# adaLN sums as a moving operand on four column groups, three more adaLN chunks on GpSimd, and the softmax scaling of head pairs placed inside the recurrence

## The chip, the cores and the metric

The kernel runs on one core of one Trainium2 chip. The metric is the device time of one execution in microseconds. A core has five engines, each with its own in-order instruction stream: TensorE (PE; its weight loads are shown as PEld), VectorE (DVE), ScalarE (ACT), GpSimd (POOL) and SyncE (SP), which here issues most of the DMAs. [...]

## The reference

One step of one trunk layer, over 1024 latent tokens and 256 context tokens, model width 1024, all in float32. The parts that the change touches:

```python
m = silu(cond) @ w_ada + b_ada                       # adaLN: 6 vectors of 1024, for two conds (c and c_ctx)
h = rms_norm(x) * (1 + sc1) + sh1
z = h @ w_in                                         # 5376 columns: recurrence, attention and gate inputs
o_a = softmax(q k^T / 8) v                           # 8 heads of 64, two kv heads; latents also see 512 cached keys
o_h = hgrn(...)                                      # gated linear recurrence, 4 heads of 128, forward and backward
merged = sigmoid(g0) * (o_h @ w_ho) + sigmoid(g1) * (o_a @ w_ao)
x = x + g1_ada * (merged @ w_out)
x = x + g2_ada * (relu(norm(x) @ w_ff1)**2 @ w_ff2)  # then a last RMSNorm
```

The six adaLN vectors need w_ada, 1024 x 6144, times two condition vectors. The softmax's division by its row sums can be done at any point between the product with v and the projection w_ao.

## The kernel before, in words

Tokens are cut in three tiles TT: t=0 and t=1 of 512 latents, t=2 of the 256 context tokens. Activations lie transposed, channels on partitions. Matrix products with weights are done as three products of high and low halves (`split` makes the halves: ACT writes the rounded one, DVE the rest; lines 312 and 313 in the profile).

The stages in order of time:

- **Front** (to about 100 us): adaLN chunks 0 to 15, first norm, the attention's own columns of w_in.
- **Attention** (to about 690 us): units of one head and 256 queries, a software pipeline of scores (L845), exponentials (L857), transposes of the probabilities (L877, split at L880) and products with v (L891, L892). Between the units' events a `Filler` runs other matmuls: ten groups of 256 columns of w_in for the recurrence, generated by `with_ada`. Six of the groups are made channel by channel (L345 to L347), four token by token (`tok`, L362 to L364). In program order the filler has reached a set share of its total, 250 us of its own estimate, at each event. A unit pair's output, two heads on 128 partitions and not yet divided by the row sums, goes to DRAM as OA[c][t], c = 0 to 3. The reciprocals of the row sums go to DRAM as RS (`sums_rows`), 80 rows.
- **Recurrence** (to about 990 us): 24 units, each a head, a direction and a tile, in the order (0,0), (0,1), (1,1), (1,0), (0,2), (1,2) of (direction, tile) for each head, so that units 0, 6, 12 and 18 are the first of a head. Loop step i does `prep` of unit i+1 (loads of uf, uq, uv, ug; two scans on DVE; products on DVE and POOL; its key product is held in `keyed`), then unit i's scores (L1122) and states (L1134), the output of unit i-1 (L1153, L1155), the transposes of unit i+1's keys (`keys_t`, L1111) and unit i-1's gate. Three more steps (LATE) end the loop. A second Filler runs the eight groups of the gates' columns of w_in between these.
- **Merge** (from about 1015 us): for the tiles in the order 0, 2, 1, loads of OH (the recurrence's outputs) and OA, the division of OA by the row sums (two row loads from RS, spread over 64 partitions each, and a DVE product, L1337), splits, then the products with w_hgrn_out and w_attn_out, gates, w_out, and the MLP.

adaLN chunks 16 to 47 are made in pairs (ci, ci+1: 256 columns of w_ada, a 1 MB load into `wraw`, a pool of two buffers). Up to ci=32, nine chunks, GpSimd multiplies and adds the eight rows of 128 (`ada_sum`, L197 to L204) into two accumulators, ACC, one for each cond; ACC exists once. Then four TensorE matmuls with the accumulators as weights and a column of ones as the moving operand add over the partitions (L210), and DVE adds the bias (L212). This happens once in each group but the first: `ada_sum` is called at 0.25 of the group's work and the matmuls at 0.90, in the last group at 0.02 and 0.42. The seven chunks from 34 on are made on TensorE alone, in the recurrence: `ada_cols` (16 matmuls, L178, an ACT copy, a transpose, L184), one after each of the first seven gate groups.

What sets the order: TensorE's instructions stand in program order. The other engines' and the DMA queues' order is laid out by a list scheduler at compile time, which may move a load or a GpSimd chain far ahead of its place in the program when its buffers and inputs are there; `high_priority` and `issue_after` bend that order. At run time each engine and queue then keeps its order. Pools: ring X has 20 tiles of 128x512 and holds, in the recurrence, uf, uq, ucp, usf, uw, uv and ug of the units under way and later the merge's `or`; PSUM has 3 banks "g", 3 "s" and 2 "t". `R`, a mask that the scans need, takes the tile of `sums` (which holds ACC[0]) after the attention.

Of the kernel before, what the change touches and what calls it, by code (L numbers as in the profile page):

```python
# [15 lines left out]
P = 128  # L16
# [28 lines left out]
def build(ctx, tc, I, O, C):  # L45
# [54 lines left out]
    def dma(out, in_):  # L100
        return sp.dma_start(out=f32(out), in_=f32(in_))
# [91 lines left out]
    def ada_sum(ci, acc):  # L193

        raw = wraw(I["w_ada"], KC, ci * P)
        w = [ada_l[:, :, c:c + 1].broadcast_to([P, KC, 256]) for c in range(2)]
        g_.tensor_tensor(acc[0], raw[:, 0], w[0][:, 0], op=ALU.mult)  # L197
        for k in range(1, KC):
            g_.tensor_tensor(acc[1], raw[:, k], w[0][:, k], op=ALU.mult)
            g_.tensor_tensor(acc[0], acc[0], acc[1], op=ALU.add)  # L200
        g_.tensor_tensor(raw, raw, w[1], op=ALU.mult)
        for n in (4, 2):
            g_.tensor_tensor(raw[:, 0:n], raw[:, 0:n], raw[:, n:2 * n], op=ALU.add)
        g_.tensor_tensor(acc[1], raw[:, 0], raw[:, 1], op=ALU.add)  # L204

        def late():
            pt = PS("t")
            for b in range(2):
                for c in range(2):
                    pe.matmul(pt[:, 2 * c + b:2 * c + b + 1], acc[c][:, b * P:(b + 1) * P], ones, start=True, stop=True)  # L210
            with tc.high_priority(offset=600):
                v.tensor_tensor(modc[:, :, ci:ci + 2], pt[:, 0:4].rearrange("p (c b) -> p c b", c=2),  # L212
                                cols[:, B_ADA + ci:B_ADA + ci + 2].unsqueeze(1).broadcast_to([P, 2, 2]), op=ALU.add)
        return late


# [701 lines left out]
    def sums_rows():  # L918
# [4 lines left out]
        s_.activation(e, pt[0:80, 0:P], AF.Copy)  # L923
        dma(RS, e)

    gone, keyed, copied = [None], [None], [None]
    q_at, o_at = {}, {}
    K = [[[None] * 4 for _ in range(2)] for _ in range(2)]
# [259 lines left out]
    def hgrn(fill, before):  # L1188

        units = [HUnit(6 * h + j, h, d, t) for h in range(4) for j, (d, t) in enumerate(((0, 0), (0, 1), (1, 1), (1, 0), (0, 2), (1, 2)))]  # L1190
        fwd = {u.h: {} for u in units}
        for u in units:
            u.fwd = fwd[u.h].get(u.t)
            fwd[u.h][u.t] = u
        N, LATE = len(units), 3

        share = [u.n + 128.0 for u in units] + [300.0] * LATE
        tot, done, st = sum(share), 0.0, None
        with tc.issue_after(gone[0].ins):
            units[0].prep()  # L1200
        before()
        units[0].keys_t()
        for i in range(N + LATE):
            part = lambda x: fill.to((done + x * share[i]) / tot)
            if i + 1 < N:
                with ExitStack() as after:
                    after.enter_context(tc.issue_after(copied[0].ins))
                    after.enter_context(tc.issue_after(keyed[0].ins))
                    units[i + 1].prep()
            if i < N:  # L1210
                u = units[i]
                part(0.25)
                u.scores(u.fwd)
                part(0.5)
                u.states_(u.st or st)
                st = u.last
                if i == 0:
                    sums_rows()
                if u.t == 2:
                    store(O["new_state_hgrn"][u.d, u.h], st)  # L1220
                part(0.75)
            if i >= LATE and units[i - LATE].d == 1:
                units[i - LATE].out_t()
            if 1 <= i <= N:
                units[i - 1].out(units[i - 1].fwd)
            part(0.95)
            if i + 1 < N:
                units[i + 1].keys_t()
            if 1 <= i <= N and units[i - 1].d == 1:
                units[i - 1].gate(units[i + 1] if i + 1 < N else None)  # L1230
            part(1.0)
            done += share[i]
# [19 lines left out]
    def with_ada(groups, ahead, behind):  # L1252

        late = []
        for i, grp in enumerate(groups):
            nxt = groups[i + 1] if i + 1 < len(groups) else None
            at, acts = 0.0, []
            if i and ahead:
                ci = ahead.pop(0)
                t0, t1 = (0.25, 0.9) if nxt else (0.02, 0.42)  # L1260
                acts = [(t0, lambda: late.append(ada_sum(ci, ACC))), (t1, lambda: late.pop()())]
            for need, n, gen in grp.stages():
                if not grp.tok and need == (0,):
                    jobs = [(0.5, lambda: grp.part(1))]
# [19 lines left out]
        if todo:  # L1284
            todo.pop()()

    fz = Filler(with_ada([*zh(0), *zh(1)], list(range(16, 34, 2)), []), 250.0)
    while pending:
        fz.add(1.0)
        flush(1.0)  # L1290
# [4 lines left out]
    gls = [Group(GL + 256 * c, gl_consume(c), False) for c in range(8)]  # L1295
    with tc.high_priority(offset=600):
        gls[0].part(0)
    fg = Filler(with_ada(gls, [], list(range(34, 48, 2))), 196.0)
    hgrn(fg, fz.rest)
    fg.rest()  # L1300
    close("sl")
# [24 lines left out]
    for t in MT:  # L1326
        n = TT[t][1]
        for c in range(8):
            r = S(name="or")
            dma(r[:, 0:n], (OH if c < 4 else OA)[c % 4][t])  # L1330
            if c >= 4:
                q = S(name="or")
                for i in range(2):
                    r0 = 10 * (2 * (c - 4) + i) + TT[t][0] // P
                    row = RS[r0:r0 + n // P, :].rearrange("(o b) p -> o (b p)", o=1)
                    dma(q[64 * i:64 * i + 64, 0:n], row.broadcast_to([64, n]))
                v.tensor_tensor(r[:, 0:n], r[:, 0:n], q[:, 0:n], op=ALU.mult)  # L1337
            oT[t][c] = hpair(t)
            split(oT[t][c][0], oT[t][c][1], r[:, 0:n])
    mg = [[None] * KC for _ in range(3)]  # L1340
# [676 lines left out]
```

## Time and profile before

| | |
|---|---|
| median of 3 runs | 2040.8 us (2040.52 to 2042.02) |
| the profiled execution's own time | 2040.07 us |
| its span | 2038.3 us |
| PE busy | 2004.0 us, 98% of the span |
| PEld busy | 1734.4 us, 85% |
| DVE busy | 1346.3 us, 66% |
| ACT busy | 940.0 us, 46% |
| POOL busy | 526.7 us, 26% |
| granted TensorE clock | 0.999 |
| DMA | 320.00 MB, mean 157 GB/s |

The span is the time from the first to the last instruction of the profiled execution. A row of the timeline gives the start, the duration, the engine, the line, the operation, output<-inputs, the shapes and how many instructions are merged in it; in brackets the idle time of the engine before it and what ended that. A row of the waits gives who waited for whom, the total in us, how often, and the longest. SPq rows are DMA issues, not transfers.

### The profile page before, as it was taken

The page shows a single profiled execution, that of the slowest core. Times are in us where ns is not written, and L with a number is a line of the kernel's source. Part 1 is how long each engine was busy: PE and PEld are TensorE (multiplying, and loading weights), DVE is VectorE, ACT ScalarE, POOL GpSimd, SP SyncE. Part 2 cuts the span into 40 slices and gives each one's busy share as a digit, 9 for nine tenths or more (in the row PEclk, how much of TensorE's full clock was granted, in tenths as well). Part 3 has the DMA queues.
Part 4 walks back from the last instruction along what each step waited for, and adds up shares of the span by engine and source line. Part 5 has one row for each costly group of instructions (what it writes and reads, how often), then busy time and mean ns, then how long its engine had stood idle before and what let it go on. Part 6 is the DMA issues. An engine that isn't in the chain of part 4 may idle for free.

```text
span 2038.3 us, 33049 instructions
## 1 busy us (share of the span) xinstructions
PE 2004.0 (98%) x12246; PEld 1734.4 (85%) x12246; DVE 1346.3 (66%) x2474; ACT 940.0 (46%) x1965; POOL 526.7 (26%) x594
## 2 busy tenths in 40 slices
PE   7899999999999999999999999999999999999998
PEld 5698889988889988888878889988888888888886
DVE  5865665655665789877355635886666666577786
ACT  4635555555565423323312335755545544333443
POOL 1471321433303655544022101222112200000120
PEclk9999999999999999999999999999999999999999
DMA  9452211322122455554844424854454489455764
GB/s 317 155 193 83 81 58 47 105 93 76 38 92 80 149 158 175 160 176 149 249 145 143 170 104 148 258 183 146 146 164 145 147 309 357 135 166 171 237 236 138
DMA packets 222626, 320.00 MB, mean 157 GB/s; under 512 B 19161, under 2 KB 140801, under 8 KB 222465
## 3 DMA queue, kind: packets, MB, share of 16 engines
q1 hardware_dynamic: 209984, 277.99, 42.8%
q0 software_dynamic: 12480, 39.91, 5.3%
q8 instruction: 96, 1.57, 0.3%
q14 instruction: 66, 0.53, 0.1%
HBM read 232.05 MB, written 85.78 MB: 156 GB/s over the span
## 4 chain that ended last, share of the span: by engine, by line
PE 90%; DMA 4%; DVE 3%; ACT 1%; issue 1%; SPq 0%; POOL 0%; POOLq 0%; DVEq 0%; ACTq 0%
PE ps_g L345 8%; PE ps_g L346 7%; PE ps_g L347 7%; PE ps_s L845 4%; PE ps_t L877 4%; PE ps_g L362 2%; PE ps_g L892 2%; PE ps_g L364 2%; PE ps_g L363 2%; PE ps_g L1804 2%; PE ps_g L1806 2%; PE ps_g L1805 2%; PE ps_g L891 2%; PE ps_s L1649 2%; PE ps_s L1651 2%; PE ps_s L1650 2%
## 5 line engine op out<-in xcount | busy, mean ns | idle before, releaser
L345 PE MATMUL ps_g<-hs,wsp 128*128 128x512 f32 (+1 forms) x896 | 322.6, 360 | 0.0
L346 PE MATMUL ps_g<-hs,wsp 128*128 128x512 f32 (+1 forms) x896 | 309.2, 345 | 2.9 <-DVE hs L313 2.9
L347 PE MATMUL ps_g<-hs,wsp 128*128 128x512 f32 (+1 forms) x896 | 309.3, 345 | 0.0
L312 ACT ACTIVATE wsp<-wraw 128x512 fp32r<-128x512 f32 (+1 forms) x186 | 116.7, 668 | 208.4 <-PE ps_g L346 81.2
L846 DVE TENSOR_REDUCE mx<-ps_s 128x1 f32<-128x512 f32 (+1 forms) x208 | 138.1, 668 | 112.6 <-PE ps_s L845 110.6
L880 DVE TENSOR_TENSOR pTl<-ps_t,pTh 128x512 fp32r<-128x512 f32 x200 | 136.4, 684 | 88.0 <-ACT pTh L880 87.6
L313 DVE TENSOR_TENSOR wsp<-wraw,wsp 128x512 fp32r<-128x512 f32 (+1 forms) x186 | 147.4, 817 | 70.0 <-ACT wsp L312 69.7
L347 PEld LDWEIGHTS ps_g<-hs,wsp 128*128 128x128 f32 x896 | 169.3, 189 | 21.7
L345 PEld LDWEIGHTS ps_g<-hs,wsp 128*128 128x128 f32 x896 | 169.6, 189 | 20.3 <-issue 4.4
L346 PEld LDWEIGHTS ps_g<-hs,wsp 128*128 128x128 f32 x896 | 169.9, 190 | 18.2 <-DVE hs L313 3.4
L880 ACT ACTIVATE pTh<-ps_t 128x512 fp32r<-128x512 f32 x200 | 118.2, 602 | 139.3 <-PE ps_t L877 137.6
L312 ACT ACTIVATE ah<-ar 128x640 fp32r<-128x640 f32 (+1 forms) x112 | 80.9, 723 | 185.9 <-PE ps_g L1805 102.3
L857 ACT ACTIVATE pexp<-ps_s,ngm 128x512 f32<-128x512 f32 (+1 forms) x208 | 137.4, 669 | 42.7 <-DVE ngm L850 42.3
L313 DVE TENSOR_TENSOR ah<-ar,ah 128x640 fp32r<-128x640 f32 (+1 forms) x112 | 92.0, 822 | 78.2 <-ACT ah L312 77.8
L845 PE MATMUL ps_s<-Kl,Ql 128*128 128x512 f32 (+1 forms) x416 | 129.5, 411 | 0.0
L877 PE MATMUL ps_t<-ident,pexp 128*128 128x128 f32 x800 | 120.0, 272 | 0.1
L362 PE MATMUL ps_g<-wsp,hs 128*128 128x256 f32 x400 | 115.8, 289 | 0.0
L364 PE MATMUL ps_g<-wsp,hs 128*128 128x256 f32 x400 | 112.9, 282 | 0.0
L363 PE MATMUL ps_g<-wsp,hs 128*128 128x256 f32 x400 | 112.6, 281 | 0.0
L892 PE MATMUL ps_g<-pTl,Vl 128*128 128x256 f32 x400 | 104.2, 283 | 0.2
L891 PE MATMUL ps_g<-pTh,Vl 128*128 128x256 f32 x400 | 104.0, 281 | 0.0
L877 PEld LDWEIGHTS ps_t<-ident,pexp 128*128 128x128 f32 x800 | 94.4, 140 | 9.5 <-issue 0.6
(436 smaller groups left out, 5363.0 us busy)
## 6 DMA issues: line engine op xcount, KB each, us to landing
ar<-AF SPq DMA_DIRECT2D x112, 320.0 KB, 3.3
wraw<-in_w_ff SPq DMA_DIRECT2D x32, 1024.0 KB, 6.4
wr<-in_w_ff SPq DMA_DIRECT2D x128, 256.0 KB, 4.4
wraw<-in_w_in SPq DMA_DIRECT2D x18, 1024.0 KB, 5.6
wraw<-in_w_ada SPq DMA_DIRECT2D x16, 1024.0 KB, 5.4
AF<-a POOLq DMA_DIRECT2D x48, 256.0 KB, 2.7
AF<-t POOLq DMA_DIRECT2D x48, 256.0 KB, 2.3
wa<-in_w_ada SPq DMA_DIRECT2D x32, 256.0 KB, 5.9
```

Source lines behind the costliest of these rows:

```text
L312: s_.activation(hi, raw, AF.Copy)
L313: return v.tensor_tensor(lo, raw, f32(hi), op=ALU.subtract)
L345: pe.matmul(out, hi[:, k, :], mh, start=(first and k == 0), stop=False)
L346: pe.matmul(out, hi[:, k, :], ml, start=False, stop=False)
L347: pe.matmul(out, lo[:, k, :], mh, start=False, stop=(last and k == kcs - 1))
L362: pe.matmul(po[:, bb, :], mh[:, off:off + P], wh[:, k % 4, :], start=(k == 0), stop=False)
L363: pe.matmul(po[:, bb, :], mh[:, off:off + P], wl[:, k % 4, :], start=False, stop=False)
L364: pe.matmul(po[:, bb, :], ml[:, off:off + P], wh[:, k % 4, :], start=False, stop=(k == KC - 1))
L845: pe.matmul(pq[:, 0:n], self.qh[:, q0:q0 + P], K[self.g][var][self.kts[i]], start=(var == 0), stop=(var == 1))
L877: pe.transpose(pt[:, a, j * P:(j + 1) * P], self.Ps[j][i][:, b * P:(b + 1) * P], ident)
L880: behind[:] = s_.activation(hi, pt, AF.Copy), v.tensor_tensor(lo, pt, f32(hi), op=ALU.subtract)
L892: pe.matmul(pv[:, 0:256], V[self.g][kg][:, b, :], lo[:, a, :], start=False, stop=(k == last))
```

## The change

It has three parts.

1. `ada_sum`'s end: the accumulators become the moving operand (128 columns) and a column of ones spread to 32 columns becomes the weights, so that the four matmuls go to four column groups of the array. The sums then lie along the columns; ACT copies them to SBUF (`ev`, 128x128), and a second step, `last`, transposes them to where the old form had them, from a "t" bank of its own, and adds the bias. `with_ada` calls the two steps apart (0.45 and 0.49, or 0.93 and 0.97 of the group).
2. GpSimd makes twelve chunks (16 to 38) instead of nine, and TensorE's `ada_cols` four (40 to 46) instead of seven: in the four token groups `with_ada` now starts a chunk at 0.02 and another at 0.50 (the last group has the first alone). The second Filler's total goes from 196 to 190.
3. The division of OA by the row sums leaves the merge. `scale_pair` loads a pair's OA tile and its two rows in every odd step of the recurrence from i=3 on, ahead of `prep` of unit i+1; its second half, in the even step after it, multiplies behind that step's `keyed` on DVE and stores the result back to OA. The twelve pairs go in the order of tiles 0, 2, 1. The merge loads OA and splits it as it does OH.

```diff
--- before.py
+++ after.py
@@ -204,13 +204,19 @@
         g_.tensor_tensor(acc[1], raw[:, 0], raw[:, 1], op=ALU.add)
 
         def late():
-            pt = PS("t")
-            for b in range(2):
-                for c in range(2):
-                    pe.matmul(pt[:, 2 * c + b:2 * c + b + 1], acc[c][:, b * P:(b + 1) * P], ones, start=True, stop=True)
-            with tc.high_priority(offset=600):
-                v.tensor_tensor(modc[:, :, ci:ci + 2], pt[:, 0:4].rearrange("p (c b) -> p c b", c=2),
-                                cols[:, B_ADA + ci:B_ADA + ci + 2].unsqueeze(1).broadcast_to([P, 2, 2]), op=ALU.add)
+            pa = PS("t")
+            for q in range(4):
+                pe.matmul(pa[32 * q:32 * q + 32, 0:P], ones.broadcast_to([P, 32]), acc[q // 2][:, (q % 2) * P:(q % 2 + 1) * P], start=True, stop=True)
+            ev = S((P, P), name="ev")
+            s_.activation(ev, pa[:, 0:P], AF.Copy)
+
+            def last():
+                pt = PS("t")
+                pe.transpose(pt[:, 0:P], ev, ident)
+                with tc.high_priority(offset=600):
+                    v.tensor_tensor(modc[:, :, ci:ci + 2], pt[:, 0:P].rearrange("p (c b x) -> p c b x", c=2, b=2)[:, :, :, 0],
+                                    cols[:, B_ADA + ci:B_ADA + ci + 2].unsqueeze(1).broadcast_to([P, 2, 2]), op=ALU.add)
+            return last
         return late
 
 
@@ -923,6 +929,21 @@
         s_.activation(e, pt[0:80, 0:P], AF.Copy)
         dma(RS, e)
 
+    def scale_pair(c, t):
+
+        n = TT[t][1]
+        r, q = S(name="or"), S(name="or")
+        dma(r[:, 0:n], OA[c][t])
+        for i in range(2):
+            r0 = 10 * (2 * c + i) + TT[t][0] // P
+            row = RS[r0:r0 + n // P, :].rearrange("(o b) p -> o (b p)", o=1)
+            dma(q[64 * i:64 * i + 64, 0:n], row.broadcast_to([64, n]))
+
+        def late():
+            v.tensor_tensor(r[:, 0:n], r[:, 0:n], q[:, 0:n], op=ALU.mult)
+            dma(OA[c][t], r[:, 0:n])
+        return late
+
     gone, keyed, copied = [None], [None], [None]
     q_at, o_at = {}, {}
     K = [[[None] * 4 for _ in range(2)] for _ in range(2)]
@@ -1200,13 +1221,19 @@
             units[0].prep()
         before()
         units[0].keys_t()
+        pairs, scaled = [(c, t) for t in (0, 2, 1) for c in range(4)], []
         for i in range(N + LATE):
             part = lambda x: fill.to((done + x * share[i]) / tot)
+            if i > 2 and i % 2 and pairs:
+                scaled.append(scale_pair(*pairs.pop(0)))
             if i + 1 < N:
                 with ExitStack() as after:
                     after.enter_context(tc.issue_after(copied[0].ins))
                     after.enter_context(tc.issue_after(keyed[0].ins))
                     units[i + 1].prep()
+            if scaled and i % 2 == 0:
+                with tc.issue_after(keyed[0].ins):
+                    scaled.pop()()
             if i < N:
                 u = units[i]
                 part(0.25)
@@ -1256,9 +1283,14 @@
             nxt = groups[i + 1] if i + 1 < len(groups) else None
             at, acts = 0.0, []
             if i and ahead:
-                ci = ahead.pop(0)
-                t0, t1 = (0.25, 0.9) if nxt else (0.02, 0.42)
-                acts = [(t0, lambda: late.append(ada_sum(ci, ACC))), (t1, lambda: late.pop()())]
+                def begin():
+                    late.append(ada_sum(ahead.pop(0), ACC))
+
+                def end():
+                    late.append(late.pop()())
+                acts = [(0.02, begin), (0.45, end), (0.49, lambda: late.pop()())] if grp.tok else []
+                if nxt:
+                    acts += [(0.5 if grp.tok else 0.25, begin), (0.93, end), (0.97, lambda: late.pop()())]
             for need, n, gen in grp.stages():
                 if not grp.tok and need == (0,):
                     jobs = [(0.5, lambda: grp.part(1))]
@@ -1284,7 +1316,7 @@
         if todo:
             todo.pop()()
 
-    fz = Filler(with_ada([*zh(0), *zh(1)], list(range(16, 34, 2)), []), 250.0)
+    fz = Filler(with_ada([*zh(0), *zh(1)], list(range(16, 40, 2)), []), 250.0)
     while pending:
         fz.add(1.0)
         flush(1.0)
@@ -1295,7 +1327,7 @@
     gls = [Group(GL + 256 * c, gl_consume(c), False) for c in range(8)]
     with tc.high_priority(offset=600):
         gls[0].part(0)
-    fg = Filler(with_ada(gls, [], list(range(34, 48, 2))), 196.0)
+    fg = Filler(with_ada(gls, [], list(range(40, 48, 2))), 190.0)
     hgrn(fg, fz.rest)
     fg.rest()
     close("sl")
@@ -1328,13 +1360,6 @@
         for c in range(8):
             r = S(name="or")
             dma(r[:, 0:n], (OH if c < 4 else OA)[c % 4][t])
-            if c >= 4:
-                q = S(name="or")
-                for i in range(2):
-                    r0 = 10 * (2 * (c - 4) + i) + TT[t][0] // P
-                    row = RS[r0:r0 + n // P, :].rearrange("(o b) p -> o (b p)", o=1)
-                    dma(q[64 * i:64 * i + 64, 0:n], row.broadcast_to([64, n]))
-                v.tensor_tensor(r[:, 0:n], r[:, 0:n], q[:, 0:n], op=ALU.mult)
             oT[t][c] = hpair(t)
             split(oT[t][c][0], oT[t][c][1], r[:, 0:n])
     mg = [[None] * KC for _ in range(3)]
```

## The prediction

> **What bounds the kernel now.** I read the page first, then PE's waits, then the timelines of the places that the diff touches.
>
> ```profile
> PE 2004.0 (98%) x12246; PEld 1734.4 (85%) x12246; DVE 1346.3 (66%) x2474; ACT 940.0 (46%) x1965; POOL 526.7 (26%) x594
> ```
> PE is busy 98% of a 2038.3 us span, so a gain is either PE work that goes or a PE wait that goes. In the table of PE's waits most are in the first 95 us, which the diff doesn't touch. Four entries bear on it:
>
> ```profile
> PE ps_g L346 <- DVE hs L313: 2.9, 2, 2.1
> ...
> PE ps_s L346 <- DVE hs L313: 0.9, 1, 0.9
> ...
> PE ps_s L1122 <- POOL usf L1073: 0.8, 1, 0.8
> PE ps_t L210 <- DVE pTl L880: 0.7, 2, 0.4
> ```
> The L346 entries (2.9 and 0.9 us, 3.8 together) lie at the start of the merge, between 1021 and 1028 us. The L210 entry is the adaLN sums waiting for a "t" bank of PSUM, and the L1122 entry all that PE lost to POOL in the recurrence. What DVE does just before the first merge wait ends:
>
> ```profile
> 1019.31 0.69 DVE L1337 TENSOR_TENSOR or<-or 128x512 f32<-128x512 f32 x1 [6.37 <-DMA or<-RS]
> 1019.92 0.42 DVE L313 TENSOR_TENSOR hs<-or,hs 128x256 fp32r<-128x256 f32 x1
> ```
> DVE idled 6.37 us for a row load of RS (the reciprocals of the softmax sums), with a 512-column scaling (0.69 us) in front of the 256-column split that PE needs. DVE is not full there; it stands in order behind a late load. SP issues such loads slowly:
>
> ```profile
> 1018.61 1.09 SPq L101 DMA_DIRECT2D or<-RS  x2
> ```
> The two RS loads of one pair take 1.09 us of the queue, and the pool that they land in (ring X, 20 tiles) must have a free tile. In stretches of the recurrence and just ahead of the merge, the engines stand so (columns: time, PE, PEld, DVE, ACT, POOL busy, clock, DMA share, GB/s):
>
> ```profile
> 775.00:800.00 25.00, 25.00 (x227) 21.19 (x226) 24.96 (x55) 7.59 (x17) 14.50 (x15) 1.00 0.56 175
> 800.00:825.00 25.00, 25.00 (x226) 22.10 (x225) 14.55 (x41) 8.29 (x24) 9.38 (x13) 1.00 0.39 125
> 1010.00:1020.00 10.00, 10.00 (x57) 8.77 (x56) 3.63 (x7) 1.69 (x4) 0.00 (x0) 1.00 1.02 302
> ```
> So the scaling leaves a stretch in which DVE works 3.63 of 10 us and POOL nothing, and goes to one where DVE is busy 24.96 of 25 us, with pauses (14.55 of 25) where the short units lie. PE's clock is 1.00 throughout.
>
> **The change, part by part.** The sums are made against the profiled execution, 2040.07 us with a span of 2038.3; the median of the runs shown, 2040.8, is 0.7 above it.
>
> *1. GpSimd's sums as moving operand.* One old chunk on PE:
>
> ```profile
> 683.25 0.28 PE L210 MATMUL ps_t<-ones,sums 128*128 128x1 f32 x2
> ...
> 684.06 0.63 PE L877 MATMUL ps_t<-ident,pexp 128*128 128x128 f32 x4
> ```
> From 683.25 to 684.06 the chunk holds PE 0.81 us: eight records, each with a full 128-column weight load. Nine chunks are 7.3 us, and the 0.7 us of bank waits above makes 8.0. The new form has the shape of the adaLN matmuls of TensorE's own chunks (32-column weights on four column groups, 128 columns moving):
>
> ```profile
> 781.88 0.28 PE L347 MATMUL ps_g<-hs,wsp 128*128 128x256 f32 x1
> 782.09 1.08 PE L178 MATMUL ps_g<-wraw,ada_l 128*32 128x128 f32 x32
> 783.10 0.66 PE L1111 MATMUL ps_t<-ident,uf 128*128 128x128 f32 x4
> ...
> ```
> Here 32 records take 1.01 us, and the step before them is 0.21 instead of the 0.12 that a 256-column record takes: 1.10 in all. Eight such records are 8/32 of 1.01, 0.25, with the same 0.09 for the change of shape: 0.34 us. The new transpose has a row too:
>
> ```profile
> 747.87 0.39 PE L347 MATMUL ps_g<-hs,wsp 128*128 128x512 f32 x1
> 748.10 0.27 PE L184 MATMUL ps_g<-ident,ev 128*128 128x128 f32 x1
> 748.13 0.48 PE L345 MATMUL ps_g<-hs,wsp 128*128 128x512 f32 x1
> 748.44 0.39 PE L346 MATMUL ps_g<-hs,wsp 128*128 128x512 f32 x1
> ```
> From 747.87 to 748.44 there are two 512-column steps of 0.23 and one transpose, which therefore costs 0.11. A new chunk is 0.45, twelve are 5.4. Each now takes two "t" banks instead of one; at 0.7 us for nine, 24 would wait 1.9 us. New total 7.3, against 8.0: **-0.7 us**. Ends: no waits -2.6; waits twice as long +1.2. The ACT copy lies between the two parts, which are 0.04 of a group apart, 1.05 us of filler work with the attention's own between: taken as hidden. If it is late as often as once a chunk, and by as much as one of the two bank waits (0.35), that is 4 us.
>
> *2. Three chunks more on GpSimd.* The chain on POOL for the last chunk:
>
> ```profile
> 661.34 0.61 POOL L197 TENSOR_TENSOR sums<-wraw,ada_l 128x256 f32<-128x256 f32 x1 [29.07 <-PE ps_t L210]
> ...
> 681.69 0.74 POOL L204 TENSOR_TENSOR pvt<-wraw 128x256 f32<-128x256 f32 x1
> ```
> It takes 21.1 us (661.34 to 682.43), and the old matmuls followed at 683.25, only 0.8 us later. Begin now comes after 0.93 instead of 0.90 of the group before, and the end at 0.45 instead of 0.42 of its own, so both move by the same 0.03 of a group. The tighter windows are those of the token groups, 0.43 of a group:
>
> ```profile
> L210 PE MATMUL ps_t<-ones,sums x36: 164/250/250, 217.2 to 683.7; 128*128 128x1 f32 x36
> ```
> From 0.90 of the second group (217.2) to 0.42 of the tenth (683.7) is 7.5 groups in 466 us, 62 us each, so a window is 27 us for a chain of 21. It fits: **0**, with 0 to 2 us for the last chunk (0.8 us of room), which is in PE's order and would hold everything behind it.
>
> *3. Three chunks less on TensorE in the recurrence.* Each is 1.10 plus 0.11 for its transpose, 1.21: **-3.6 us**, if PE remains the bound there; 0 if it must wait for DVE instead. The budget of the filler is cut by 6, three times the 1.8 that a chunk yielded, so the spread of the gate groups stays.
>
> *4. Scaling out of the merge.* Twelve multiplications and 24 RS loads go ahead of the merge; 12 stores and 12 loads of OA are new, and each pair in the recurrence costs SP an OA load, two RS loads and a store, about 2 us of queue by the row above (1.09 for two). The merge keeps 24 loads and 24 splits. Eight tiles for t=0 and eight for t=2 then fit in 20 tiles of ring X at once, so no split stands behind a late row load: **-3.8 us**; ends 0 (the splits are then late for another reason) and -3.8. The 0.69 that each multiplication takes there comes back as DVE idle time, worth nothing.
>
> *5. Scaling into the recurrence.* Here is what I take to be its price. Each pair holds two tiles of ring X from its loads to the landing of its store, over an iteration and more. The loads are placed before the preparation of an even unit, and units 6, 12 and 18, the first of a head, are even. When SP issued the uf loads of the first two:
>
> ```profile
> 753.18 0.32 SPq L101 DMA_DIRECT2D uf<-FD  x1
> ...
> 821.47 0.57 SPq L101 DMA_DIRECT2D uf<-FD  x1
> ```
> When PE released tiles and when it wanted the keys (L1111 is the transposes of keys, four or two per unit; L1122 is the scores):
>
> ```profile
> 755.52 0.27 PE L1122 MATMUL ps_s<-uq,usf 128*32 128x128 f32 x1
> ...
> 769.30 0.60 PE L1111 MATMUL ps_t<-ident,uf 128*128 128x128 f32 x4
> ...
> 821.06 0.38 PE L1111 MATMUL ps_t<-ident,uf 128*128 128x128 f32 x2
> ...
> 824.05 0.27 PE L1122 MATMUL ps_s<-uq,usf 128*32 128x128 f32 x1
> ...
> 837.13 0.60 PE L1111 MATMUL ps_t<-ident,uf 128*128 128x128 f32 x4
> ...
> 890.78 0.27 PE L1122 MATMUL ps_s<-uq,usf 128*32 128x128 f32 x1
> ...
> 905.20 0.60 PE L1111 MATMUL ps_t<-ident,uf 128*128 128x128 f32 x4
> ```
> and when DVE had the keys ready (L1073 uf):
>
> ```profile
> 766.87 0.68 DVE L1073 TENSOR_TENSOR uf<-usf,um 128x512 f32<-128x512 f32 x1
> ...
> 833.94 1.22 DVE L1307 SCALAR_TENSOR_TENSOR s<-modc,cols 128x8 f32<-128x8 f32 x1
> ...
> 835.17 1.21 DVE L1073 TENSOR_TENSOR uf<-usf,um 128x512 f32<-128x512 f32 x1
> ...
> 903.99 0.68 DVE L1073 TENSOR_TENSOR uf<-usf,um 128x512 f32<-128x512 f32 x1
> ```
> Unit 12: its load went out at 821.47, as the transposes of unit 10 ended (821.06+0.38) and released a tile. With two tiles less it waits for the next release, the four tiles that the scores give back at 824.32: 2.85 us later. The multiplication stands on DVE in the same stretch, 0.69. Its keys were ready at 836.38 and wanted at 837.13: 0.75 of room; and L1307 (1.22, the scale of the second norm) goes from in front of them, since its chunks now end in the attention. 2.85+0.69-0.75-1.22 = 1.6. Unit 6: 753.18 to 755.79, 2.6, plus 0.69, less room of 1.75 (767.55 to 769.30): 1.5. Unit 18 has two rows more, its load in the chain that ended last and the median of all uf loads from issue to landing:
>
> ```profile
> 889.15 5.82 DMA uf<-FD
> ```
> ```profile
> uf<-FD SPq DMA_DIRECT2D x16, 256.0 KB, 3.3
> ```
> It is later by 1.9 (889.15 to 891.05), less 0.53 of room (904.67 to 905.20): 1.4; but the load took 5.82 against a median of 3.3, so a later start may land no later: 0. Sum **+3.1 us**. Ends: 0 (the tiles are there) and 20, worked out below; near the low end, because PE lost only the 0.8 us of the L1122 row to this stage so far.
>
> [...]
>
> ```profile
> L1073 DVE TENSOR_TENSOR uw<-uq,um x24: 411/678/1505, 694.7 to 955.9; 128x512 f32<-128x512 f32 x16, 128x256 f32<-128x256 f32 x8
> ```
> The same kind of product of two SBUF tiles takes 0.68 in the median and up to 1.51 beside POOL. [...] In the merge POOL did nothing, so the old place was free of it.
>
> Sum: -0.7 + 0 - 3.6 - 3.8 + 3.1 = -5.0. 2040.07 - 5.0 = 2035.1, and 0.7 more for the median: **2035.8 us**.
>
> **Rivals.**
> *A, no change: DVE is the bound of the recurrence.* If each of the twelve multiplications delays PE by its median of 0.68, that is 8.2 us instead of 3.1: -0.7-3.6-3.8+8.2 = +0.1, 2040.9. For it: 24.96 of 25 us. Against: 10 us of pause in the next 25, and PE lost only 0.8 us to this stage before.
> *B, slower: tiles run out.* If the tiles of two pairs are held at once, four are missing, and the whole release at the scores is used up. The next tile that comes free for unit 12 is that of the output gate (L1177 reads ug):
>
> ```profile
> 828.50 1.05 DVE L1177 SCALAR_TENSOR_TENSOR uo<-uo,orst,ug 128x128 f32<-128x128 f32 x4
> ```
> It ends at 829.55, 8.1 us after the old issue. Taken for all three, less the room of 1.75, 0.75 and 0.53, that is 6.3+7.3+7.6 = 21.2, less 1.2 for L1307 20 us: -8.1+20 = +11.9, 2052.7. It makes the kernel slower from 4.1 us per first unit on, where the three take 12. Against: a pair's store should have landed before the next pair's loads.
> *C, slower: each multiplication meets POOL.* POOL is busy 14.50 of 25 us in the full stretch. If every multiplication waits out one of its instructions and PE waits with it, each costs the row's maximum, 1.51, and twelve 18 us: -8.1+18 = +10, 2051. Against: the median of the row. [...]
> *D, no change: the merge keeps its waits.* The splits of t=2 can't begin before PE has read the last gate group; if DVE's other splits are then in front, the 3.8 stay: 2039.6.
>
> **How the numbers follow.** A change of under 0.2% (4.1 us) can't be told from none. Forecast, 2031 to 2037: 0.56, of which a little lies above 2036.7. A 0.20, D 0.12, B 0.08, C 0.04. Faster 0.54, the same 0.34, slower 0.12. The low end, 2031, is the sum without part 5 (-8.1) and without bank waits; the high end, 2041, takes in A and D. B and C are left out.
>
> **What would show it.** After: L346 without waits at the start of the merge; twelve new adaLN chunks of about 0.45 us on PE, without a wait for POOL; four chunks of TensorE's own in the recurrence; and waits of 1 to 2 us at the key transposes or scores of units 6 and 12. The prediction is wrong if PE waits for POOL in the attention, if DVE or ring X holds more than the three first units, or if waits at the merge remain.

## The result and the profile after

After: **2053.9 us** median (2052.89 to 2056.08), beside 2041.41 us for the kernel before on the same chip: a ratio of 1.006, 95% interval 1.0042 to 1.0077, slower by 12.5 us. The forecast was 2035.8. The profiled execution took 2056.08 us, its span 2054.2; it is the slowest of the four, so its stages lose 15.9 us and not 12.5.

The page's line of busy times, which was PE's 2004.0 of 2038.3 us before:

```profile
PE 2008.0 (98%) x12183; PEld 1732.3 (84%) x12183; DVE 1344.8 (65%) x2471; ACT 942.3 (46%) x1974; POOL 582.8 (28%) x651
```

PE is busy 4.0 us more in a span 15.9 us longer: most of the loss is waiting. The stages by the starts of PE's instructions in the two timelines (us):

| stage | before | after |
|---|---|---|
| start to first transpose of the attention | 169.05 | 171.36 |
| attention, to unit 0's keys | 532.98 | 533.13 |
| recurrence, to unit 23's state matmuls | 267.86 | 283.51 |
| from there to the transpose of the gate columns `gc`, in the merge | 63.85 | 59.78 |
| rest | 1004.57 | 1006.47 |

The first and the last stage are not touched by the diff; over all kernels profiled here they vary by 4.1 and 2.7 us. So the recurrence lost 15.7 us, the merge gained 4.1 and the attention stood still. As the kernels come to the recurrence at different times, places in it are compared below by their distance from unit 0's keys (702.03 before, 704.49 after). PE's waits between 640 and 1040 us, after:

```profile
PE ps_s L1155 <- issue: 9.9, 3, 5.2
PE ps_t L1132 <- DVE uf L1094: 3.8, 3, 1.8
```

The merge's waits (now L352) are gone. The L1132 entry is the three first units that the prediction priced, 3.8 us for 3.1; unit by unit it is 1.0, 1.0 and 1.8 for 1.5, 1.6 and 0, so the sum agrees better than its parts. The L1155 entry, state matmuls that wait, was in no term. Around unit 7 of the after kernel, PE's timeline:

```profile
789.79 0.39 PE L353 MATMUL ps_g<-hs,wsp 128*128 128x512 f32 x1
794.66 2.04 PE L1155 MATMUL ps_s<-uv,ukt 128*128 128x128 f32 x8 [4.47 <-issue]
...
797.35 0.63 PE L353 MATMUL ps_g<-hs,wsp 128*128 128x512 f32 x1
797.78 0.63 PE L351 MATMUL ps_g<-hs,wsp 128*128 128x512 f32 x1
...
799.76 0.40 PE L353 MATMUL ps_g<-hs,wsp 128*128 128x512 f32 x1
799.99 0.40 PE L351 MATMUL ps_g<-hs,wsp 128*128 128x512 f32 x1
```

PE pauses for 4.47 us, and then it is slow: from 797.35 to 797.78 a 512-column step takes 0.43 us, from 799.76 to 799.99 again 0.23. The windows around this pause and around the second one (5.2 us, unit 19), where the page before had a clock of 1.00:

```profile
775.00:800.00 25.00, 20.27 (x187) 17.42 (x188) 19.82 (x43) 5.88 (x14) 11.84 (x13) 0.86 0.74 229
925.00:950.00 25.00, 19.81 (x129) 16.69 (x128) 19.13 (x44) 4.75 (x12) 8.70 (x10) 0.86 0.54 168
```

The granted clock falls to 0.86 in both. From the transposes of unit 7's keys to those of unit 8's it is 18.42 us where it was 11.22, and 20.17 for 12.51 at unit 19: 7.2 and 7.7 us, of which 4.5 and 5.2 are the pauses and about 2.5 each the slow clock. The two make 14.9 of the 15.7.

What unit 7 waited for is seen on SP. Before, the uf load of unit 8 went out at 772.49, DVE scanned it at 778.26 without a wait for it, and the state updates of unit 6 (`ust`) that stand behind that scan in DVE's order ended at 785.74, 2.5 us before PE's state matmuls of unit 7:

```profile
772.49 0.32 SPq L101 DMA_DIRECT2D uf<-FD  x1
```
```profile
778.26 1.21 DVE L1051 TENSOR_TENSOR_SCAN ucp<-R,uf 128x512 f32<-128x512 f32 x1
...
785.02 0.72 DVE L1143 SCALAR_TENSOR_TENSOR ust<-ust,udec,ps_s 128x128 f32<-128x128 f32 x2
```
```profile
788.28 1.05 PE L1134 MATMUL ps_s<-uv,ukt 128*128 128x128 f32 x8
```

After, SP's queue, with its waits in these 17 us in the second view:

```profile
780.20 0.32 SPq L101 DMA_DIRECT2D or<-OA  x1
...
784.46 0.51 SPq L101 DMA_DIRECT2D uf<-FD  x1
...
790.48 0.56 SPq L101 DMA_DIRECT2D uv<-VD  x1
```
```profile
SPq L101 <- DVE um L1104: 5.5, 1, 5.5
SPq L101 <- DMA OA<-or: 4.2, 1, 4.2
SPq L101 <- DVE udec L1107: 2.1, 1, 2.1
```

The pair's OA load stands first and waits 5.5 us until a tile of ring X comes free (um L1104 reads it last); its first RS load waits 2.1 more. uf stands behind them and goes out at 784.46, 80.0 us behind unit 0's keys where it was 70.5: 9.5 us later. Then, on DVE:

```profile
789.14 1.23 DVE L1072 TENSOR_TENSOR_SCAN ucp<-R,uf 128x512 f32<-128x512 f32 x1 [4.67 <-DMA uf<-FD]
...
793.84 0.72 DVE L1164 SCALAR_TENSOR_TENSOR ust<-ust,udec,ps_s 128x128 f32<-128x128 f32 x2
```

DVE stands idle 4.67 us for uf, with the state updates of unit 6 queued behind the scan. They end at 794.56 (793.84+0.72), and PE's state matmuls start 0.1 us later: they need one of the three PSUM banks "s", and the updates read one of them. At the same place uv of unit 7 had been held 4.2 us for the landing of the pair's store, whose tile it takes over, and was issued only at 790.48. Two candidates for one wait; the experiments separate them.

At unit 19 the chain is the same, from an OA load that stood 10.4 us at the head of SP's queue to the scan, but its last link is another:

```profile
931.96 1.23 DVE L1072 TENSOR_TENSOR_SCAN ucp<-R,uf 128x512 f32<-128x512 f32 x1 [4.82 <-DMA uf<-FD]
...
940.16 0.42 DVE L1187 TENSOR_TENSOR uo<-ps_s,uo 128x256 f32<-128x256 f32 x1
```
```profile
940.68 1.62 PE L1155 MATMUL ps_s<-uv,ukt 128*128 128x128 f32 x6 [5.19 <-issue]
```

PE starts 0.1 us behind `uo` (L1187, ends at 940.58), which takes unit 17's output out of its bank, and before the last update of unit 18 has begun (941.10). So what holds the bank is work of DVE behind the late scan, at one place an update and at the other this sum.

### The profile page after: what moved, and what is told of

Read it like the earlier page. It is cut to its first block, busy times and chain, and to the rows that moved or that the text cites. A ratio compares the mean times of both kernels' runs of the same rounds, so it can differ in the third digit from the quotient of the medians.

```text
span 2054.2 us, 33070 instructions
## 1 busy us (share of the span) xinstructions
PE 2008.0 (98%) x12183; PEld 1732.3 (84%) x12183; DVE 1344.8 (65%) x2471; ACT 942.3 (46%) x1974; POOL 582.8 (28%) x651
## 4 chain that ended last, share of the span: by engine, by line
PE 89%; DVE 4%; DMA 3%; ACT 1%; issue 1%; SPq 1%; POOL 0%; POOLq 0%; ACTq 0%; DVEq 0%
PE ps_g L351 7%; PE ps_g L353 7%; PE ps_g L352 7%; PE ps_s L851 5%; PE ps_t L883 4%; PE ps_g L368 2%; PE ps_g L1831 2%; PE ps_g L898 2%; PE ps_g L1829 2%; PE ps_g L1830 2%; PE ps_g L370 2%; PE ps_g L897 2%; PE ps_g L369 2%; PE ps_s L1674 2%; PE ps_s L1676 2%; PE ps_s L1675 2%
## 5 line engine op out<-in xcount | busy, mean ns | idle before, releaser
L352 PE MATMUL ps_g<-hs,wsp 128*128 128x512 f32 (+1 forms) x896 | 310.4, 346 | 0.0
L319 DVE TENSOR_TENSOR wsp<-wraw,wsp 128x512 fp32r<-128x512 f32 (+1 forms) x186 | 152.8, 846 | 93.7 <-ACT wsp L318 93.3
L352 PEld LDWEIGHTS ps_g<-hs,wsp 128*128 128x128 f32 x896 | 170.9, 191 | 15.1
L164 POOL TENSOR_TENSOR frst<-ms,mexp 128x1 f32<-128x1 f32 x10 | 11.4, 1151 | 321.8 <-DVE ssf L1918 278.4
```

Source lines behind the costliest of these rows:

```text
L319: return v.tensor_tensor(lo, raw, f32(hi), op=ALU.subtract)
L352: pe.matmul(out, hi[:, k, :], ml, start=False, stop=False)
```

## The experiments

Theory S: PE waits for uv, hence for the landing of the store that holds its tile. Theory O: PE waits for the updates, which are late because the pair's loads stand ahead of the next unit's in SP's queue. In the expectations, T is that only the number of free tiles counts, and A that the adaLN parts themselves cost time; this A is not the prediction's rival A (DVE as the bound). Every kernel was timed beside runs of the kernel before, whose medians were 2042.24 (first four), 2040.73 (next four) and 2042.87 us (last three).

**Parts 1 and 2 alone.** The division stays in the merge, as before.

```diff
-        pairs, scaled = [(c, t) for t in (0, 2, 1) for c in range(4)], []
+        pairs, scaled = [], []
+ # ... merge: RS loads and product as in the kernel before
```

> Parts 1 and 2 alone; the scaling is back in the merge. Theory S (the loss comes from two loads of uv that wait on SP for the landing of the store of OA, because they take over its tile of ring X): no such store exists here, so the two waits of 4.5 and 5.2 us and the slow clock after them are gone; PE keeps the merge waits of 3.8 and loses the work of three chunks, 3.6: 2037 to 2039. Rival A (the adaLN parts themselves cost time: the after kernel is already 2.3 us late when the attention begins): 2042 to 2044. Rival T (only the number of free tiles matters): as S.

Measured: 2038.5 us, ratio 0.9981 (0.9972 to 0.9989), 3.9 us faster. The recurrence took 263.23 us, 4.6 less than before; of the merge's waits 2.4 of 3.8 us stay. So A falls; the sums and the chunks together are worth what terms 1 to 3 said (-4.3), and time taken from PE in the recurrence shows in full: DVE isn't its bound.

**Part 3 alone**, on the kernel before.

```diff
+ # ... scale_pair and its calls in hgrn, as in the change; ada_sum, with_ada, the chunks as before
```

> Part 3 alone on the kernel before. In the order of SP's queue only one load of uv (the one of unit 19) now waits for a store of OA, instead of three (units 7, 13 and 19). S: one jump of about 7.6 us at unit 19 and none at unit 7, 2 to 4 us of waits at the first units of the heads, the merge waits of 3.8 gone: 2046 to 2049. T (two tiles fewer, whoever holds them): both jumps, 2053 to 2056. A: 2042 to 2045 at most, since the adaLN parts are not in it.

Measured: 2056.05 us, ratio 1.0062 (1.0049 to 1.0075). The whole loss is in part 3, and more than S expected; the time is T's, but the place is neither's. PE doesn't pause at units 7 and 19 but at the keys of units 6 and 12:

```profile
PE ps_t L1126 <- DVE uf L1088: 9.1, 2, 5.0
```
```profile
756.59 0.33 SPq L101 DMA_DIRECT2D or<-OA  x1
...
760.61 0.38 SPq L101 DMA_DIRECT2D uf<-FD  x1
```

The picture on SP is that of unit 8: OA and RS ahead of uf, which for unit 6 goes out 57.8 us behind unit 0's keys (702.78) where it was 51.2.

**Product in a tile of ring J.** The store no longer holds a ring X tile.

```diff
+            w = S(name="or", ring="J")
-            v.tensor_tensor(r[:, 0:n], r[:, 0:n], q[:, 0:n], op=ALU.mult)
-            dma(OA[c][t], r[:, 0:n])
+            v.tensor_tensor(w[:, 0:n], r[:, 0:n], q[:, 0:n], op=ALU.mult)
+            dma(OA[c][t], w[:, 0:n])
```

> The after kernel, with the product of the scaling written to a tile of ring J, which nobody else needs then, so that the two tiles of ring X are free when DVE has multiplied and not when the store has landed. The order of SP's queue in the recurrence is the same; the three loads of uv wait for PE instead of the store. S: both jumps (7.2 and 7.7 us) go, the waits at the first units of the heads stay: 2037 to 2040. T: the loads wait as long for PE's release: 2051 to 2055.

Measured: 2052.12 us, ratio 1.005 (1.0038 to 1.0062). S falls. Counted from unit 0's keys (703.18), uv goes out 4.1 us earlier and nothing else moves: uf is as late (80.1 us behind them), DVE as idle, PE's pause as long. The time is what T expected.

```profile
783.26 0.51 SPq L101 DMA_DIRECT2D uf<-FD  x1
...
785.11 0.56 SPq L101 DMA_DIRECT2D uv<-VD  x1
```
```profile
788.00 1.22 DVE L1073 TENSOR_TENSOR_SCAN ucp<-R,uf 128x512 f32<-128x512 f32 x1 [4.72 <-DMA uf<-FD]
```
```profile
793.51 1.87 PE L1156 MATMUL ps_s<-uv,ukt 128*128 128x128 f32 x8 [4.52 <-issue]
```

**Ring J, and the pair's loads behind the next unit's.**

```diff
-            if i > 2 and i % 2 and pairs: scaled.append(...)   # ahead of units[i + 1].prep()
+            if i > 2 and i % 2 and pairs: scaled.append(...)   # behind it
```

> As the kernel with the product in ring J, and the pair's three loads are placed behind the preparation of the next unit instead of ahead of it. S with the tile argument of the prediction (first units of a head start late because the pair takes tiles first): the 3.8 us of waits at the key transposes of units 6, 12 and 18 shrink to 1 or less, 2034 to 2037. If those waits come from DVE's extra product instead, they stay: 2037 to 2040.

Measured: 2040.49 us, ratio 0.999 (0.9982 to 0.9999): 11.6 us back against the version before it. Neither range of the text holds the time: of the waits at the first units one stays, 1.4 us at unit 12, and small ones came elsewhere. No pause above 1.4 us is left in the recurrence; it takes 268.20 us, and the merge keeps its gain (59.92).

**The same order, product in ring X again.** Ring J is undone, the loads stay behind the next unit's.

> Theory O (order): the loss comes from the place of a pair's three loads ahead of the next unit's loads in SP's queue, so that this unit's uf is late, DVE waits for it in order, and the state updates behind it come late. Only the three loads are moved behind that unit's loads; the product stays in a ring X tile and is stored from there. O: the uf of units 8 and 20 is issued 3 to 6 us earlier than in the changed kernel, PE's pauses at units 7 and 19 are under 2 us, the clock stays at 1.00, and the time is 2038 to 2043 us. Rival J (the product's ring): the order alone isn't enough, because uv of the same unit still takes the tile that the store holds; then a pause of 3 to 5 us at units 7 and 19 stays and the time is 2047 to 2053 us.

Measured: 2039.24 us, ratio 0.9992 (0.9983 to 1.0). The order alone does it:

```profile
772.03 0.85 SPq L101 DMA_DIRECT2D uf<-FD  x1
```
```profile
777.90 2.05 DVE L1072 TENSOR_TENSOR_SCAN ucp<-R,uf 128x512 f32<-128x512 f32 x1 [0.15 <-DMA uf<-FD]
```

uf of unit 8 goes out at 772.03, 70.5 us behind unit 0's keys (701.58) as before, and DVE waits 0.15 us for it. The clock stays at 1.00. Rival J falls, and T with it: a pair takes its two tiles as in the change.

**The pair's loads on ACT's queue**, at their old place ahead of the next unit's.

```diff
-        dma(r[:, 0:n], OA[c][t])
+        s_.dma_start(out=f32(r[:, 0:n]), in_=OA[c][t])     # ... both RS loads likewise
```

> The changed kernel, with a pair's three loads issued by ACT's queue in place of SP's, at the same place of the program: they still take two tiles of ring X ahead of the next unit's loads, but SP's queue no longer holds them. If SP's three issues and their waits make uf late (the queue): uf of unit 8 is issued about 4 us earlier than 784.46, and the time is 2038 to 2044 us. If the two tiles make it late (the ring): uf is issued no more than 1.5 us earlier, because its own tile is the third one on and comes free only after um and udec of the unit before; then PE's pauses of 4 to 5 us stay and the time is 2048 to 2056 us. ACT waits for the same tiles in order, and the copies of keys stand behind it; that can add 2 to 6 us in either case and would show as PE waits on ACT.

Measured: **2034.12 us**, ratio 0.9967 (0.9955 to 0.9979). That is below both ranges of the text. SP's queue has no load of a pair in it:

```profile
775.56 0.33 ACTq L936 DMA_DIRECT2D or<-OA  x1
```
```profile
776.98 0.37 SPq L101 DMA_DIRECT2D uf<-FD  x1
```

uf goes out at 776.98, 74.6 us behind unit 0's keys (702.42): 5.4 us earlier than in the after kernel and still 4.1 later than before. SP's wait ahead of it, 3.9 us, is now for ACT's copy `ze`, which stands behind the pair's OA load in ACT's order; how much of that the two tiles cause isn't shown. PE has room for it. Of the waits on ACT that the text expected, PE's table has 0.2 us.

**State updates ahead of the scan.** The ring J version, with DVE's order changed and no load moved; this is the direct test of how a late uf reaches PE.

```diff
+                    if i > 2 and i % 2 and upd[0]:      # upd[0]: the last update issued
+                        after.enter_context(tc.issue_after(upd[0].ins))
                     units[i + 1].prep()
```

> The version with the product in ring J (2052.1 us; there uv of units 7 and 19 is early and uf of units 8 and 20 is still late), with the scan of each even unit put behind the state updates of the unit two before it in DVE's order, at the steps that issue a pair's loads. Theory O's second half says that PE's pauses at units 7 and 19 are a PSUM bank held by state updates that stand behind a scan that waits for uf. Then the updates of unit 6 end at 785 to 789 us in place of 793.4, the pauses of 4.5 and 5.7 us shrink below 2 us, the clock stays at 1.00 there, and the time is 2040 to 2045 us; some of the loss stays, as the keys of units 8 and 20 are still late. Rival K (keys): PE would wait for the late keys of units 8 and 20 as long as it waits now for the bank, 4 us or more at their transposes, and the time stays at 2049 to 2054 us.

Measured: 2045.29 us, ratio 1.0019 (1.0011 to 1.0028), where the ring J version had 1.005: some 6 us better.

```profile
784.65 1.11 DVE L1165 SCALAR_TENSOR_TENSOR ust<-ust,udec,ps_s 128x128 f32<-128x128 f32 x3
789.80 1.23 DVE L1073 TENSOR_TENSOR_SCAN ucp<-R,uf 128x512 f32<-128x512 f32 x1 [4.03 <-DMA uf<-FD]
```
```profile
PE ps_t L1133 <- DVE uf L1095: 5.6, 4, 1.9
```

uf is as late (scan at 789.80, after 4.03 us of waiting), but the updates of unit 6 end at 785.76 and the pauses of 4.5 and 5.7 us are gone. That holds at unit 19 too, where `uo`, which had stood behind updates and two weight splits, ends at 933.79: 4.2 us behind the start of the scan instead of 8.6. What remains are four waits for late keys, up to 1.9 us, and one of 1.6 at the state matmuls of unit 20, which start 0.1 us behind an update. Rival K falls for the two pauses; it holds for most of the rest. Two of these short waits slowed PE too. On its timeline behind the longest:

```profile
913.21 0.63 PE L1133 MATMUL ps_t<-ident,uf 128*128 128x128 f32 x4 [1.87 <-DVE uf L1095]
...
914.39 0.63 PE L351 MATMUL ps_g<-hs,wsp 128*128 128x512 f32 x1
914.82 0.63 PE L352 MATMUL ps_g<-hs,wsp 128*128 128x512 f32 x1
```

The step is 0.43 from 914.39 to 914.82, and the granted clock 0.73 from 915 to 920; the wait of 1.30 us at unit 8's keys was followed by the same (0.43 from 799.37 to 799.80, a clock of 0.83 from 800 to 805).

**Four pairs alone.** Of the version with ring J and late loads, only the pairs of tile t=0, at steps 13, 15, 19 and 21.

```diff
-        pairs, scaled = [(c, t) for t in (0, 2, 1) for c in range(4)], []
+        pairs, scaled = [(c, 0) for c in range(4)], []      # ... called for i in (13, 15, 19, 21)
+            if c >= 4 and t:  # ... merge: RS loads and product as in the kernel before
```

> As the version with the product in ring J and the loads behind the next unit's, but only the four pairs of token tile 0 are scaled in the recurrence (at steps 13, 15, 19 and 21, away from the first units 6, 12 and 18); the eight others are scaled in the merge, as in the kernel before. Theory O says that each pair in the recurrence costs DVE and SP time that PE sees only at first units, and that the merge's 3.8 us of waits come from the first token tile alone: the recurrence then ends 2 to 3 us earlier than with twelve pairs, the merge's waits stay gone, and the time is 2035 to 2038.5 us, under the 2038.5 of the sums alone. Rival M: the merge waits for the other two token tiles instead (row loads of RS ahead of their splits), and the time is 2038 to 2042 us.

Measured: **2033.91 us**, ratio 0.9965 (0.9953 to 0.9977). That is below the range of the text. The recurrence is 3.2 us shorter than with twelve pairs (265.04 for 268.20), and in the merge one wait of 0.5 us stays, so that the merge's waits came from the first token tile and rival M falls.

**Four pairs with their loads on ACT's queue**, product in ring X.

> The four pairs of token tile 0 alone in the recurrence, as in the version of 2033.9 us, but with the pair's loads on ACT's queue ahead of the next unit's loads and the product in its ring X tile, as in the version of 2034.1 us. If the two gains (fewer pairs; SP's queue free of them) are of one kind, nothing is left to add: 2033 to 2035 us. If each pair still costs the recurrence about 0.1 us by ring X, this one loses the same as the other: no difference either. A result under 2032 us would say that the loads cost SP's queue time even behind the next unit's loads.

Measured: **2033.81 us**, ratio 0.9958 (0.9944 to 0.9971). Its profile has the shortest span of all, 2031.5, but the intervals of the three best versions overlap.

**Long and short pauses made on purpose.** The four-pair version, with eight or four extra DVE products that read the bank ahead of the state updates of units 6 and 18.

> The version with four pairs in the recurrence (2033.9 us), with eight extra 512-column products of DVE (about 0.7 us each, read from the PSUM bank and thrown away) ahead of the state updates of units 6 and 18 alone. It holds the bank that unit 7 and 19 need, with no change to a load. If a held bank is what stopped PE: PE pauses of 4 to 6 us before the state matmuls of units 7 and 19. If the clock falls after such a pause whatever made it: granted clock 0.8 to 0.9 in the 25 us around each, 512-column steps of about 0.43 us for some 6 us, and 2 to 3 us lost at each beyond the pause. Rival: the clock fell for another reason (the load of the transfers then), and it stays at 1.00 here.

> As the one before with four products in place of eight: pauses of about 2 us at units 7 and 19. If there is a length under which the clock stays, as the pauses of 1 to 2 us at the first units of a head said: granted clock 1.00 and steps of 0.23 us right behind the pauses, and the recurrence ends later by no more than the pauses themselves (3 to 5 us).

Measured, one run each: 2053.17 and 2036.8 us. With eight, PE waits twice, but not where the text expected: unit 7's state matmuls start at 787.74, while the products still read unit 6's bank, and the pauses come behind them, at the outputs (L1179) of units 6 and 18:

```profile
PE ps_s L1179 <- DVE usf L1075: 5.6, 1, 5.6
PE ps_s L1179 <- DVE usm L1148: 5.2, 1, 5.2
```
```profile
797.16 0.79 PE L1179 MATMUL ps_s<-s,uw 128*128 128x128 f32 x2 [5.60 <-DVE usf L1075]
...
800.95 0.63 PE L352 MATMUL ps_g<-hs,wsp 128*128 128x512 f32 x1
801.38 0.57 PE L353 MATMUL ps_g<-hs,wsp 128*128 128x512 f32 x1
...
802.46 0.39 PE L352 MATMUL ps_g<-hs,wsp 128*128 128x512 f32 x1
802.69 0.40 PE L353 MATMUL ps_g<-hs,wsp 128*128 128x512 f32 x1
```
```profile
925.00:950.00 25.00, 19.66 (x148) 16.38 (x147) 22.98 (x47) 5.81 (x14) 9.85 (x10) 0.86 0.28 86
```

The first pause ends 0.05 us behind DVE's product `usm` (L1148, 796.45 + 0.66), to which the second is put down too and which reads the scores' bank: a bank that DVE holds too long again, but another one. The clock falls just as after the pauses of the change: 0.86 over the 25 us around the second, 512-column steps of 0.43 from 800.95 to 801.38, and 0.23 from 802.46 on, 5.3 us behind the end of the pause. No transfer was changed, so the pause by itself does it. With four, the products were hidden in DVE's room and there was no pause above 0.8 us in the recurrence; that run says nothing of lengths.

Each pause of 4.1 to 5.7 us here came with a lower granted clock, 0.83 to 0.93 in the window of 20 or 25 us in which it ended, and where the rows behind it were read, with steps of 0.43 us: behind 4.47 and 5.19 us in the after kernel, 4.09 in part 3 alone (775.59 to 776.02), 4.52 with the product in ring J (795.61 to 796.04) and 5.60 in the run with eight products. Shorter ones went either way. With the updates put first, 1.30 and 1.87 us were followed by such steps, while 1.6 us at unit 20 left the clock at 1.00 (940 to 960), and so did 1.83 us in the after kernel (unit 18, 1.00 from 900 to 925, steps of 0.23 behind it). So length alone doesn't tell these apart; what does isn't shown.

## Why the prediction was wrong, point by point

- *Term 1, the sums as moving operand (-0.7).* 0 within 0.2: the attention took 533.13 us for 532.98. The bank waits are gone, but a chunk costs more than the 0.45 taken. The step into it is 0.21 and the one out of it 0.23, where 0.12 is usual and the forecast counted the first alone; its eight records take 0.35 instead of 0.25. The last one (the others are within 0.01 of it):

```profile
687.29 0.28 PE L370 MATMUL ps_g<-wsp,hs 128*128 128x256 f32 x1
687.50 0.30 PE L209 MATMUL ps_t<-sums,ones 128*32 128x128 f32 x2
...
687.85 0.39 PE L368 MATMUL ps_g<-wsp,hs 128*128 128x256 f32 x1
688.08 0.28 PE L369 MATMUL ps_g<-wsp,hs 128*128 128x256 f32 x1
```

  From 687.29 to 688.08 are 0.79 us with two 0.12 steps in it, 0.55, and about 0.1 for the transpose: 0.65, twelve of them 7.8 us for the 8.0 before.
- *Term 2, three chunks more on GpSimd (0).* Right here: no wait for POOL in the attention. The last chunk's room is small, as the prediction said: with four pairs and their loads on ACT's queue, PE waited 0.5 us for it.
- *Term 3, three chunks fewer (-3.6).* Right in kind, somewhat small: -4.6 in the recurrence of the first experiment.
- *Term 4, the merge (-3.8).* Right: -4.1, without a wait.
- *Term 5, the scaling in the recurrence (+3.1): the step that failed.* The waits that it priced came (3.8 us), and the two pauses that it didn't see cost 14.9; beside the first experiment's 263.23, part 3 costs the recurrence 20.3 us, of which some 1.6 aren't placed. The prediction's own sign of being wrong came: DVE held more than the three first units. For unit 18 it leaves out the multiplication's 0.69 that units 6 and 12 have and then counts nothing; that unit lost 1.8. Three things were left out. First, term 4 counted some 2 us of SP's queue for a pair and term 5 never charged them, nor that the loads themselves wait for a tile at the head of the queue (5.5 and 2.1 us at unit 8) with uf behind them. Second, it asked when the keys are wanted, at first units alone. The scan also holds what stands behind it on DVE, the state updates and the output's sum, and one of these holds a bank that PE needs sooner; at unit 7 the room was 2.5 us, readable in three rows of before (778.26, 785.02, 788.28). Third, a pause was taken at its length, where those of 4.5 and 5.2 us at units 7 and 19 cost 7.2 and 7.7.
- *The sum.* With the pairs' loads on ACT's queue the change gives 0.9967, that is -6.7 us for the -5.0 forecast; with them on SP's queue behind the next unit's, 0.9992 or -1.6. Four pairs give -7.1 and -8.6, near the -8.1 without term 5.
- *Rival B (tiles run out, 2052.7)* has the time, but not the mechanism: it put 6 to 8 us at each of units 6, 12 and 18, which lost 1 to 1.9, and the loss lay at units 7 and 19. With the tiles as scarce as in the change and only the order of the loads changed, the loss is gone. That its time is near the measured one is luck. Nearest to it comes part 3 alone, where units 6 and 12 lost 4.1 and 5.0 us; no run changes the order there.
- *Rival C (each multiplication meets POOL)* is refuted by the multiplications' own row, a maximum of 0.693 us, though a product of POOL ran beside ten of the twelve, begun 0.16 us behind them:

```profile
L943 DVE TENSOR_TENSOR or<-or x12: 414/682/693, 756.2 to 986.1; 128x512 f32<-128x512 f32 x8, 128x256 f32<-128x256 f32 x4
```

- *Rival A* is refuted by the first experiment (PE's saved time shows in full); the twelve pairs on ACT's queue cost the recurrence 4.0 us (267.21 for 263.23), not 8.2. *D* is refuted by the merge.

Two points stay open. The parts don't add up: -3.9 and +12.7 make 8.8, the two together lost 12.5; the pauses fall at other units in each, and why there wasn't followed. The version with the loads behind the next unit's stands 5 us above the one with the loads on ACT's queue; their recurrences differ by 1.7 us (268.92 and 267.21). The rest can't be placed, as their profiled executions differ by 0.5 us alone (2036.47, the lowest of eleven, and 2035.95, the highest of five).

## What to carry to other kernels

A load that has to wait for a free buffer makes everything behind it in an in-order queue wait too (at unit 8 the OA load waited 5.5 us on SP and its first RS load 2.1 more, and uf behind them went out 9.5 us later): put such a load behind the loads that the critical engine needs next, or on a queue where nothing urgent follows. When a load gets later, follow it through the whole order of the engine that waits for it: what stands behind the wait may free a bank that is needed sooner than the load's own result (at unit 7 DVE stood idle 4.67 us for uf, and PE 4.47 us for the updates behind it). And move only as much work as the gain needs: four of the twelve pairs carried nearly the whole gain of the merge.

## What was unexpected of the hardware

In the after kernel each of the two long pauses of PE, 4.47 and 5.19 us, cost some 2.5 us more than its length: behind it 512-column steps took 0.43 us for 0.23, at a granted clock of 0.86 over the 25 us around it. Waits of 1.30 and 1.87 us, with the updates put first, were followed by the same steps, one of 1.83 us in the after kernel was not; what sets them apart isn't shown. And a change of shape on PE, from 128-column to 32-column weights and back, cost 0.09 us on the way in (a step of 0.21 for 0.12) and 0.11 on the way out (0.23 for 0.12), where the forecast had counted the first alone.
